# A decoder block on one core: the arithmetic of the early and attention parts moved from GpSimd to VectorE and ScalarE

## The chip, the core and the metric

The kernel runs on one core of a Trainium2 chip. The core has four engines that compute, each with its own instruction queue that it works through in order: TensorE (PE in the profile; its weight loads are a row of their own, PEld), VectorE (DVE), ScalarE (ACT) and GpSimd (POOL). SyncE (SP) issues most transfers. The metric is the device time of one execution in microseconds (us), the median of several runs. One more execution was taken by the profiler; all rows below are of that one.

## The reference, cut to what matters

One decoder block on 256 tokens of width 2048, in float32. Only the first half of it, the token mixer, is touched by the change:

```python
h = rms_norm(x, g_pre_mix) * (1.0 + sc1) + sh1        # sc1, sh1, ... = silu(c) @ w_ada + b_ada
z = h @ w_in                                          # cq, ckv, kr, qs, ks, vs and two gates
o_a = mla_branch(cq, ckv, kr, g_q_lat, w_uq, g_kv_lat, w_ukv)   # 16 heads, rotary part, causal
o_b = swa_branch(qs, ks_, vs, rel_bias, sinks)                  # 32 heads of 64, window 128, sinks
mix = (g_a * o_a + g_b * o_b) @ w_o
x = x + gt1 * rms_norm(mix, g_post_mix)
# then: u = causal_dwconv((rms_norm(x) * (1 + sc2) + sh2) @ w_up); y = (silu(u1) * u2) @ w_down
# apply_rope(x) = x * cos + rotate_half(x) * sin; softmax with a sink adds exp(sink - m) to the sum
```

## The kernel before

Every float32 matrix product is made of three products of rounded halves. A weight tile `raw` of 128 x 1024 arrives by transfer; ACT rounds it to `whi` (L116), DVE subtracts to get the rest `wlo` (L117), and PE multiplies hi by hi, hi by lo and lo by hi (`mm3`, L129 to L131, and variants to L146). Five buffers each of `raw`, `whi` and `wlo` stand between the transfers and PE. The other operand is split in the same way.

The program has these stages. **Early columns** (`early_z`): z for the latents, the keys, the values and the first heads is made in six groups of the 2048 input channels (`KGS` = 2, 2, 2, 2, 4, 4 chunks of 128); the sums over the groups stay in SBUF as twenty tiles `pair` of 128 x 512. For the first group ACT copies a finished PSUM bank (`bk_mm`, three of them) to the pair. For the later ones every third pair (index mod 3 = 1, `PADD`) is copied out by ACT (L373) and added by POOL (L374); the others are added by DVE straight from PSUM (L376). Beside it, modulation columns are made in a background stream: w_ada tiles are multiplied by silu(c) on PE or summed up on DVE (`acc`, L240 and L242). **Hooks in the last group**: `lat` normalises the two latents (sums of squares, L406 on POOL; split, L421 on POOL), `keys` rotates the shared key and splits the keys (L448 to L456 on POOL), `toeplitz` prepares the bias. **Attention**, for eight pairs of heads: `pair_proj` projects queries, keys and values from the latents, and `rope` rotates the queries of two pairs at a time: four products with the sine on 32 partitions each (L434, POOL), one with the cosine (L435, DVE), one sum (L436, POOL). `step` runs one head of MLA and two of the window branch. `stack` puts hi of a 64-row operand on one half of the partitions (L464, ACT) and lo on the other (L465, POOL). Scores go to two PSUM banks (`bk_sc`, L545 to L550); DVE adds mask or bias, takes the maximum and writes to `sm` (L555, two per bank); ACT takes the exponential with its sum (L561); DVE inverts the sum (L563) and multiplies (L566, six per head); PE transposes (L150), ACT copies out (L574), PE multiplies by the values (L578, L583); DVE gates (L586), POOL adds the two branches (L589). `late_z` makes the remaining columns in between. Then come w_o, the second norm, the ConvFFN and the end, which the change doesn't touch.

The order on each engine is fixed before the run: the source calls `tile.TileContext(nc, schedule_with_timeline_sim=True)`, and a scheduler places the instructions of all engines by its own account of them. So a change of engine also moves other instructions in the queues.

Of the kernel before, what the change touches and what calls it, by code (L numbers as in the profile page):

```python
# [10 lines left out]
F32 = mybir.dt.float32  # L11
F32R = mybir.dt.float32r
AF = mybir.ActivationFunctionType
ALU = mybir.AluOpType

P = 128
# [9 lines left out]
NEARLY = 8  # L26
LATS = (3, 4, 5, 6, 7, 8, 9)
HOOKS = (3, 9, 15)
PADD = 3
PUMP = 1.3  # L30
RATES = (0.5, 0.8, 0.3, 0.5)
SPREAD = 7.0
# [11 lines left out]
def block_kernel(ctx: ExitStack, tc: tile.TileContext, a, out: bass.AP):  # L44
# [295 lines left out]
    def early_z(kg, hooks):  # L340
        s, k0 = KGS[kg], k0s[kg]
        nblk = 2048 // (s * P)
        order = []
        for i in range(NPAIR):
            order += [("kr", 6)] if i == 6 else [("vs", 7), ("vs2", 7)] if i == 7 else [(0, i), (1, i)]
        src = a["w_in1"][kg]
        b = None
        for off in range(0, len(order), nblk):
            n = min(nblk, len(order) - off)
            w = n * P * s  # L350
            wt = Weights(src[:, off * P * s:off * P * s + w], w, WT if n == nblk else n * P * (s // 2))
            for u in range(n):
                what, i = order[off + u]
                if what in (0, "kr", "vs"):
                    b = bank("mm")
                if what == "vs":
                    for half in range(2):
                        for kk in range(s):
                            mm3t(b[:, half * T:half * T + T], wt.cut(kk * n * P + u * P, 2 * P), hs[k0 + kk], half,
                                 kk == 0, kk == s - 1)  # L360
                elif what != "vs2":
                    c0 = T if what == 1 else 0
                    for kk in range(s):
                        mm3(b[:, c0:c0 + T], wt.cut(kk * n * P + u * P), hs[k0 + kk], kk == 0, kk == s - 1)
                if what in (1, "kr", "vs2"):
                    wd = T if i == 6 else 2 * T
                    if kg == 0:
                        pairs[i] = blkp.tile([P, 512], F32, tag="blk", name="pair")
                        act.copy(pairs[i][:, :wd], b[:, :wd])
                    elif i % PADD == 1:  # L370
                        pl = xp if kg < len(KGS) - 1 else at
                        part = pl.tile([P, 512], F32, tag="sq" if pl is xp else "tmp", bufs=2, name="part")
                        act.copy(part[:, :wd], b[:, :wd])  # L373
                        pool.tensor_tensor(pairs[i][:, :wd], pairs[i][:, :wd], part[:, :wd], op=ALU.add)  # L374
                    else:
                        dve.tensor_tensor(pairs[i][:, :wd], pairs[i][:, :wd], b[:, :wd], op=ALU.add)  # L376
                    if i in hooks:
                        hooks[i]()
# [19 lines left out]
    def lat(first, npair, width, gofs, res):  # L398
# [4 lines left out]
        for i in range(1, npair):  # L403
            sq = at.tile([P, 512], F32, tag="tmp", name="sq2")
            act.activation(sq, pairs[first + i], AF.Square)
            pool.tensor_tensor(tot, tot, sq, op=ALU.add)  # L406
        for j in range(2):
            pe.matmul(ps[:, :T], ones, tot[:, j * T:j * T + T], start=j == 0, stop=j == 1)
        r = at.tile([P, 512], F32, tag="ropet", bufs=1, name="rl")[:, :T]
# [2 lines left out]
        for i in range(npair):  # L412
# [5 lines left out]
            hi = blkp.tile([P, 512], F32R, tag="blk", name="blk_hi")  # L418
            lo = blkp.tile([P, 512], F32R, tag="blk", name="blk_lo")
            act.copy(hi, pr)  # L420
            pool.tensor_tensor(lo, pr, hi.bitcast(F32), op=ALU.subtract)  # L421
            res += [(hi[:, j * T:j * T + T], lo[:, j * T:j * T + T], None) for j in range(2)]

    def rope(x, n):
# [6 lines left out]

        for q in range(4):
            here, there = slice(32 * q, 32 * q + 32), slice(32 * (q ^ 1), 32 * (q ^ 1) + 32)
            pool.tensor_tensor(t[here], x[there], table(sinT, there), op=ALU.mult)  # L434
        dve.tensor_tensor(x, x, table(cosT, slice(0, P)), op=ALU.mult)  # L435
        pool.tensor_tensor(x, x, t, op=ALU.add)  # L436

    cqn, ckn = [], []

# [3 lines left out]
    def keys():  # L443
# [1 line left out]
        krr = pairs[6][:, :T]  # L445
        rope(krr, 1)
        act.copy(krs[:, 0, :], krr)
        pool.tensor_tensor(krs[:, 1, :], krr, krs[:, 0, :].bitcast(F32), op=ALU.subtract)  # L448
        ksf = at.tile([P, 3, 388], F32, tag="sm", bufs=2, name="ksf").rearrange("p a b -> p (a b)")[:, :4 * T]
        for kv in range(4):  # L450
            src = pairs[5][(kv % 2) * 64:(kv % 2) * 64 + 64, (kv // 2) * T:(kv // 2) * T + T]
            for i in range(2):
                pool.tensor_scalar(down_order(ksf[64 * i:64 * i + 64, kv * T:kv * T + T]), src, -0.125, None, op0=ALU.mult)
        hi = kss[:, 0].rearrange("p k t -> p (k t)")
        act.copy(hi, ksf)
        pool.tensor_tensor(kss[:, 1].rearrange("p k t -> p (k t)"), ksf, hi.bitcast(F32), op=ALU.subtract)  # L456

    def stack(src, tag, w):

# [2 lines left out]
        for e in range(2):  # L462
            me, other = slice(64 * e, 64 * e + 64), slice(64 - 64 * e, 128 - 64 * e)
            act.copy(res[e][me], src[me])  # L464
            pool.tensor_tensor(res[e][other], src[me], res[e][me].bitcast(F32), op=ALU.subtract)  # L465
        return res


# [52 lines left out]
    def step(h):  # L521
# [36 lines left out]
        for i in range(3):  # L558
# [4 lines left out]
            dve.reciprocal(den[:, 2 * i:2 * i + 2], den[:, 2 * i:2 * i + 2])  # L563
            for j, (c0, c1) in enumerate(SEG):
                o, r = sm[:, i, c0:c1], den[:, 2 * i + j:2 * i + j + 1]
                dve.tensor_scalar(o, o, r, None, op0=ALU.mult)  # L566
        ob = bank("o")
        pts = []
        for i in range(3):
# [16 lines left out]
        dve.scalar_tensor_tensor(tm, tg, 1.0, ob, op0=ALU.add, op1=ALU.mult)  # L586
        if e == 0:
            mixs[h // 2] = blkp.tile([P, 512], F32, tag="blk", name="mix")
        pool.tensor_tensor(mixs[h // 2][:, e * T:e * T + T], tm[:, 0:T], tm[:, T:512], op=ALU.add)  # L589

    warm = const.tile([P, 1], F32, name="warm")

# [324 lines left out]
```

## Time and profile before

| | before |
|---|---|
| median of 3 runs | 1502.75 us (1501.55 to 1503.86) |
| profiled execution | 1505.71 us, of which the span 1503.8 us |
| PE busy | 1452.7 us, 97% of the span |
| PEld busy | 1278.0 us, 85% |
| DVE busy | 1083.8 us, 72% |
| ACT busy | 775.6 us, 52% |
| POOL busy | 260.9 us, 17% |
| mean granted clock of PE | 0.988 |

The span is the stretch from the first to the last instruction. The shares are means over stages of different kinds: the early columns last to about 250 us, the last group with its hooks and the attention to about 650 us, and w_o, the norm and the ConvFFN take the rest. A busy PE is modelled from its pipelined matmuls, so 100% is no proof of its peak. The granted clock is the share of TensorE's full speed that the chip allowed.

### The profile page before, as it was taken

What the parts mean: (1) busy time and instruction counts of PE and PEld (TensorE: products, weight loads), DVE (VectorE), ACT (ScalarE), POOL (GpSimd) and SP (SyncE); (2) the same over time, 40 slices, a digit from 0 to 9 for tenths busy, and PEclk for the clock granted to TensorE, in tenths of its full rate; (3) what the DMA queues carried; (4) which work ended last, traced back from release to release, by engine and by line L of the source; (5) the groups of instructions that cost most, each with busy time, mean ns of one, the idle gap of its engine ahead of it and who ended that gap; (6) DMA issues with size and microseconds to landing.
All of it is one profiled execution on the core that took longest, in us unless ns stands there. A gap on an engine that the chain in (4) does not pass through costs nothing.

```text
span 1503.8 us, 24728 instructions
## 1 busy us (share of the span) xinstructions
PE 1452.7 (97%) x9506; PEld 1278.0 (85%) x9506; DVE 1083.8 (72%) x1488; ACT 775.6 (52%) x1223; POOL 260.9 (17%) x191
## 2 busy tenths in 40 slices
PE   7999999889999999999899989999999999999997
PEld 6988899789899998978788878888888888888886
DVE  3579868978887969767788777877767776444443
ACT  4534435545554655755655445655555555434442
POOL 0034315922413425300000000100000000000000
PEclk9999999999999999999899999999999999999999
DMA  9888868588687867659477777765555557555552
GB/s 373 312 313 323 311 233 266 180 272 271 201 298 235 301 228 259 202 201 388 178 243 251 239 253 266 251 209 190 187 190 189 189 190 242 193 195 190 191 193 99
DMA packets 101525, 356.96 MB, mean 237 GB/s; under 512 B 11760, under 2 KB 12208, under 8 KB 100896
## 3 DMA queue, kind: packets, MB, share of 16 engines
q1 hardware_dynamic: 99936, 350.82, 68.4%
q0 software_dynamic: 1472, 4.58, 1.2%
q8 instruction: 74, 1.21, 0.3%
q14 instruction: 43, 0.35, 0.1%
HBM read 351.11 MB, written 4.24 MB: 236 GB/s over the span
## 4 chain that ended last, share of the span: by engine, by line
PE 38%; DMA 10%; DVE 5%; ACT 1%; issue 1%; SPq 0%; DVEq 0%; ACTq 0%
PE bk_mm L136 8%; PE bk_sc L136 6%; DMA raw<-in_w_ada_dram 6%; PE bk_mm L138 4%; PE bk_sc L138 3%; PE bk_mm L144 3%; PE bk_sc L144 3%; PE bk_sc L146 3%; PE bk_mm L146 3%; PE bk_mm L145 3%; PE bk_sc L145 3%; DMA raw<-in_w_up_dram 2%; DVE acc L242 2%; DMA raw<-in_w_o_dram 2%; DVE wlo L117 2%
## 5 line engine op out<-in xcount | busy, mean ns | idle before, releaser
L117 DVE TENSOR_TENSOR wlo<-raw,whi 128x1024 fp32r<-128x1024 f32 (+3 forms) x472 | 594.3, 1266 | 282.8 <-ACT whi L116 280.7
L116 ACT CAST whi<-raw 128x1024 fp32r<-128x1024 f32 (+3 forms) x472 | 478.3, 1021 | 504.8 <-PE bk_mm L130 91.2
L129 PE MATMUL bk_mm<-h,whi 128*128 128x256 f32 x976 | 284.3, 292 | 0.5 <-DVE pair L376 0.5
L131 PE MATMUL bk_mm<-h,wlo 128*128 128x256 f32 x976 | 279.3, 287 | 0.0
L130 PE MATMUL bk_mm<-h,whi 128*128 128x256 f32 x976 | 279.1, 286 | 0.0
L136 PE MATMUL bk_mm<-h,whi 128*128 128x512 f32 x848 | 266.6, 396 | 1.2 <-ACT whi L116 1.2
L242 DVE SCALAR_TENSOR_TENSOR acc<-raw,csil,acc 128x1024 f32<-128x1024 f32 (+1 forms) x141 | 192.1, 1362 | 57.9 <-DMA raw<-in_w_ada_dram 57.3
L129 PEld LDWEIGHTS bk_mm<-h,whi 128*128 128x128 f32 x976 | 187.9, 193 | 16.0 <-issue 11.6
L138 PEld LDWEIGHTS bk_mm<-h,wlo 128*128 128x128 f32 x848 | 158.7, 188 | 44.8 <-DVE wlo L117 7.8
L130 PEld LDWEIGHTS bk_mm<-h,whi 128*128 128x128 f32 x976 | 188.3, 193 | 1.7 <-issue 1.7
L131 PEld LDWEIGHTS bk_mm<-h,wlo 128*128 128x128 f32 x976 | 187.8, 193 | 1.4 <-issue 1.3
L136 PE MATMUL bk_sc<-h,whi 128*128 128x512 f32 x560 | 177.1, 398 | 0.0
L138 PE MATMUL bk_mm<-h,wlo 128*128 128x256 f32 x848 | 167.4, 279 | 4.8 <-DVE wlo L117 4.8
L136 PEld LDWEIGHTS bk_mm<-h,whi 128*128 128x128 f32 x848 | 129.2, 189 | 1.9 <-ACT whi L116 1.4
L138 PEld LDWEIGHTS bk_sc<-h,wlo 128*128 128x128 f32 x560 | 105.4, 189 | 27.3 <-DVE wlo L117 2.6
L761 POOL TENSOR_TENSOR sa<-sa,u 128x512 f32<-128x512 f32 x22 | 33.4, 1520 | 472.8 <-DVE u L755 436.6
L138 PE MATMUL bk_sc<-h,wlo 128*128 128x256 f32 x560 | 110.6, 279 | 1.6 <-DVE wlo L117 1.6
L374 POOL TENSOR_TENSOR pair<-pair,part 128x512 f32<-128x512 f32 x35 | 64.5, 1843 | 190.2 <-ACT part L373 190.1
L136 PEld LDWEIGHTS bk_sc<-h,whi 128*128 128x128 f32 x560 | 85.7, 190 | 0.4 <-issue 0.4
L144 PE MATMUL bk_sc<-whi,g 128*128 128x512 f32 x176 | 68.6, 390 | 0.0
L144 PE MATMUL bk_mm<-whi,g 128*128 128x512 f32 x176 | 68.6, 390 | 0.0
L145 PE MATMUL bk_mm<-wlo,g 128*128 128x512 f32 x176 | 68.5, 389 | 0.0
(197 smaller groups left out, 2261.1 us busy)
## 6 DMA issues: line engine op xcount, KB each, us to landing
raw<-in_w_ada_dram SPq DMA_DIRECT2D x192, 512.0 KB, 5.1
raw<-in_w_up_dram SPq DMA_DIRECT2D x176, 512.0 KB, 4.6
raw<-in_w_in_dram SPq DMA_DIRECT2D x116, 512.0 KB, 5.2
raw<-in_w_down_dram SPq DMA_DIRECT2D x88, 512.0 KB, 4.5
raw<-in_w_o_dram SPq DMA_DIRECT2D x32, 512.0 KB, 5.7
raw<-in_w_uqn_dram SPq DMA_DIRECT2D x16, 384.0 KB, 4.0
bias<-trow POOLq DMA_DIRECT2D x16, 256.0 KB, 4.9
raw<-in_w_ukv_dram SPq DMA_DIRECT2D x16, 256.0 KB, 3.6
```

The costliest lines, as they stand in the source:

```text
L116: act.copy(hi[:, :n], raw[:, :n])
L117: dve.tensor_tensor(lo[:, :n], raw[:, :n], hi[:, :n].bitcast(F32), op=ALU.subtract)
L129: pe.matmul(o, wh, xh, start=start, stop=False)
L130: pe.matmul(o, wh, xl, start=False, stop=False)
L131: pe.matmul(o, wl, xh, start=False, stop=stop)
L136: pe.matmul(o, w[0], x[2], start=start and i == 0, stop=False)
L138: pe.matmul(o[:, :T], w[1], x[0], start=False, stop=stop and i == 1)
L144: pe.matmul(o, ch, wh, start=start, stop=False)
L145: pe.matmul(o, ch, wl, start=False, stop=False)
L146: pe.matmul(o, cl, wh, start=False, stop=stop)
L242: dve.scalar_tensor_tensor(acc[:, :w], r, csil[:, j:j + 1], acc[:, :w], op0=ALU.mult, op1=ALU.add)
L374: pool.tensor_tensor(pairs[i][:, :wd], pairs[i][:, :wd], part[:, :wd], op=ALU.add)
```

## The change

All arithmetic that POOL did up to the end of the attention goes to other engines. The third of the partial sums that took ACT and POOL is now made like the others, by one DVE instruction out of PSUM (so the copies of L373 are gone). The sums of squares, the lo halves of latents and keys, the sine products and sums of the rotation, the stacks' lo halves and the sums of the two branches are now DVE instructions of the same shape. The eight scaled copies in `keys` and the last three of each head's six normalising products go to ACT. POOL keeps the copies of the sinks, its transfers and the product in the ConvFFN (L761).

```diff
-PADD = 3
@@ early_z
-                    elif i % PADD == 1:
-                        pl = xp if kg < len(KGS) - 1 else at
-                        part = pl.tile([P, 512], F32, tag="sq" if pl is xp else "tmp", bufs=2, name="part")
-                        act.copy(part[:, :wd], b[:, :wd])
-                        pool.tensor_tensor(pairs[i][:, :wd], pairs[i][:, :wd], part[:, :wd], op=ALU.add)
                     else:
                         dve.tensor_tensor(pairs[i][:, :wd], pairs[i][:, :wd], b[:, :wd], op=ALU.add)
@@ lat
-            pool.tensor_tensor(tot, tot, sq, op=ALU.add)
+            dve.tensor_tensor(tot, tot, sq, op=ALU.add)
-            pool.tensor_tensor(lo, pr, hi.bitcast(F32), op=ALU.subtract)
+            dve.tensor_tensor(lo, pr, hi.bitcast(F32), op=ALU.subtract)
@@ rope
-            pool.tensor_tensor(t[here], x[there], table(sinT, there), op=ALU.mult)
+            dve.tensor_tensor(t[here], x[there], table(sinT, there), op=ALU.mult)
         dve.tensor_tensor(x, x, table(cosT, slice(0, P)), op=ALU.mult)
-        pool.tensor_tensor(x, x, t, op=ALU.add)
+        dve.tensor_tensor(x, x, t, op=ALU.add)
@@ keys
-        pool.tensor_tensor(krs[:, 1, :], krr, krs[:, 0, :].bitcast(F32), op=ALU.subtract)
+        dve.tensor_tensor(krs[:, 1, :], krr, krs[:, 0, :].bitcast(F32), op=ALU.subtract)
-                pool.tensor_scalar(down_order(ksf[...]), src, -0.125, None, op0=ALU.mult)
+                act.mul(down_order(ksf[...]), src, -0.125)
-        pool.tensor_tensor(kss[:, 1].rearrange("p k t -> p (k t)"), ksf, hi.bitcast(F32), op=ALU.subtract)
+        dve.tensor_tensor(kss[:, 1].rearrange("p k t -> p (k t)"), ksf, hi.bitcast(F32), op=ALU.subtract)
@@ stack
-            pool.tensor_tensor(res[e][other], src[me], res[e][me].bitcast(F32), op=ALU.subtract)
+            dve.tensor_tensor(res[e][other], src[me], res[e][me].bitcast(F32), op=ALU.subtract)
@@ step
-                dve.tensor_scalar(o, o, r, None, op0=ALU.mult)
+                if 2 * i + j < 3:
+                    dve.tensor_scalar(o, o, r, None, op0=ALU.mult)
+                else:
+                    act.mul(o, o, r)
-        pool.tensor_tensor(mixs[h // 2][:, e * T:e * T + T], tm[:, 0:T], tm[:, T:512], op=ALU.add)
+        dve.tensor_tensor(mixs[h // 2][:, e * T:e * T + T], tm[:, 0:T], tm[:, T:512], op=ALU.add)
```

The changed file is shorter, so its line numbers are lower by one (`wlo` is L116 there, `acc` L241) and from `early_z` on by six (L376 becomes L370, L465 becomes L459, L555 becomes L549); the products of L566 are L561 on DVE and L563 on ACT.

How the queues changed is shown at two places. The first is DVE's queue in the last group of early columns, where the latents are normalised (`rl` is the inverse norm, L417 the product with it). Before:

```order
L117 TENSOR_TENSOR wlo<-raw,whi 128x1024
L242 SCALAR_TENSOR_TENSOR acc<-raw,csil,acc 128x1024
L117 TENSOR_TENSOR wlo<-raw,whi 128x768
L411 RECIPROCAL rl<-rl 128x256
L376 TENSOR_TENSOR pair<-pair,bk_mm 128x512
L417 SCALAR_TENSOR_TENSOR pair<-pair,c_gcol,rl 128x256 x4
L117 TENSOR_TENSOR wlo<-raw,whi 128x768
L242 SCALAR_TENSOR_TENSOR acc<-raw,csil,acc 128x1024
```

Now, between the same two pieces of work:

```order
L116 TENSOR_TENSOR wlo<-raw,whi 128x1024 x2
L370 TENSOR_TENSOR pair<-pair,bk_mm 128x512
L405 RECIPROCAL rl<-rl 128x256
L459 TENSOR_TENSOR qs<-pair,qs 64x512
L241 SCALAR_TENSOR_TENSOR acc<-raw,csil,acc 128x1024
L459 TENSOR_TENSOR qs<-pair,qs 64x512
L415 TENSOR_TENSOR blk_lo<-pair,blk_hi 128x512
L370 TENSOR_TENSOR pair<-pair,bk_mm 128x512
L116 TENSOR_TENSOR wlo<-raw,whi 128x1024
L116 TENSOR_TENSOR wlo<-raw,whi 128x768
L370 TENSOR_TENSOR pair<-pair,bk_mm 128x512
L411 SCALAR_TENSOR_TENSOR pair<-pair,c_gcol,rl 128x256 x4
```

The first stacks, a lo half and more of the partial sums, which stood in POOL's queue, are now between the inverse norm and the product with it. The second place is DVE's queue at the second rotation, with the reductions of the next scores (`c_cmask` those of MLA, `bias` those of the window branch; each is two instructions, of which the second reads out the maximum). Before:

```order
L117 TENSOR_TENSOR wlo<-raw,whi 128x1024 x3
L242 SCALAR_TENSOR_TENSOR acc<-raw,csil,acc 128x1024
L555 ISA sm,mx<-bk_sc,c_cmask,c_sink_97 128x128
L555 ISA mx 128x1
L555 ISA sm,mx<-bk_sc,c_cmask,c_sink_97 128x256
L555 ISA mx 128x1
L435 TENSOR_TENSOR ropeq<-ropeq,c_cosT 128x512
L555 ISA sm,mx<-bk_sc,bias,c_sink_97 128x128
```

Now:

```order
L241 SCALAR_TENSOR_TENSOR acc<-raw,csil,acc 128x1024
L428 TENSOR_TENSOR ropet<-ropeq,c_sinT 32x512 x4
L116 TENSOR_TENSOR wlo<-raw,whi 128x1024
L241 SCALAR_TENSOR_TENSOR acc<-raw,csil,acc 128x1024
L429 TENSOR_TENSOR ropeq<-ropeq,c_cosT 128x512
L116 TENSOR_TENSOR wlo<-raw,whi 128x1024
L549 ISA sm,mx<-bk_sc,bias,c_sink_97 128x128
L549 ISA mx 128x1
L549 ISA sm,mx<-bk_sc,bias,c_sink_97 128x256
L549 ISA mx 128x1
L241 SCALAR_TENSOR_TENSOR acc<-raw,csil,acc 128x1024
L430 TENSOR_TENSOR ropeq<-ropeq,ropet 128x512
```

The four sine products stand ahead of the reductions, and the closing sum behind the first two of them.

## Rows read from the trace of the kernel before

**Rows 1.** The chain of work that ended last, in order of time, its earliest piece: start and length in us, what.

```profile
677.38 11.84 DMA raw<-in_w_o_dram
```

**Rows 2.** Busy time of each engine in stretches of the span: stretch, its length, then for each engine busy us and number of instructions, the granted clock of PE, the share of the transfer engines and GB/s.

```profile
50.00:250.00 200.00, 200.00 (x1771) 182.11 (x1772) 155.88 (x193) 87.90 (x116) 60.02 (x33) 1.00 0.83 290
100.00:150.00 50.00, 50.00 (x430) 44.33 (x429) 45.84 (x54) 21.08 (x28) 21.32 (x11) 1.00 0.91 340
250.00:300.00 50.00, 43.26 (x337) 41.96 (x335) 46.65 (x41) 28.85 (x41) 46.84 (x33) 0.97 0.64 197
300.00:350.00 50.00, 43.87 (x340) 42.64 (x341) 41.64 (x60) 27.58 (x55) 16.22 (x12) 0.93 0.81 276
350.00:400.00 50.00, 46.35 (x354) 43.43 (x353) 42.22 (x77) 25.52 (x54) 18.24 (x16) 0.97 0.75 245
400.00:650.00 250.00, 244.85 (x1910) 227.80 (x1910) 207.48 (x387) 141.18 (x310) 81.03 (x66) 0.99 0.75 247
```

The engines stand in the order PE, PEld, DVE, ACT, POOL.

**Rows 3.** What PE waited for from 250 to 650 us: us in total, times, the longest.

```profile
PE bk_sc L550 <- DVE mx L555: 10.5, 5, 4.0
PE bk_mm L129 <- DVE pair L376: 5.2, 4, 2.6
PE bk_mm L145 <- DVE wlo L117: 2.2, 1, 2.2
PE bk_mm L131 <- DVE wlo L117: 1.4, 2, 1.0
PE bk_tp L150 <- DVE sm L566: 1.3, 3, 0.6
```

**Rows 4.** Groups of POOL's instructions over the whole span, shapes apart: line, operation, out<-in, count, then busy us, mean ns of one, and the idle time before them with what ended it.

```profile
L374 POOL TENSOR_TENSOR pair<-pair,part 128x512 f32<-128x512 f32 x35 | 64.5, 1843 | 190.2 <-ACT part L373 190.1
...
L434 POOL TENSOR_TENSOR ropet<-ropeq,c_sinT 32x512 f32<-32x512 f32 x16 | 32.3, 2017 | 34.2 <-ACT ropeq L502 33.5
L465 POOL TENSOR_TENSOR qs<-pair,qs 64x512 fp32r<-64x512 f32 x16 | 27.7, 1734 | 32.1 <-ACT qs L464 31.7
L589 POOL TENSOR_TENSOR mix<-tm 128x256 f32<-128x256 f32 x16 | 21.8, 1365 | 81.1 <-DVE tm L586 81.1
L465 POOL TENSOR_TENSOR qr<-ropeq,qr 64x256 fp32r<-64x256 f32 x16 | 16.5, 1032 | 62.0 <-ACT qr L464 61.5
...
L456 POOL TENSOR_TENSOR kss<-ksf,kss 128x1024 fp32r<-128x1024 f32 x1 | 3.3, 3265 | 0.1
```

**Rows 5.** The same view of DVE from 0 to 250 us.

```profile
L117 DVE TENSOR_TENSOR wlo<-raw,whi 128x1024 fp32r<-128x1024 f32 x59 | 76.4, 1315 | 26.6 <-ACT whi L116 25.8 <-DMA raw<-in_w_in_dram 0.6
L376 DVE TENSOR_TENSOR pair<-pair,bk_mm 128x512 f32<-128x512 f32 x51 | 34.4, 681 | 15.6 <-PE bk_mm L131 15.3
L242 DVE SCALAR_TENSOR_TENSOR acc<-raw,csil,acc 128x1024 f32<-128x1024 f32 x18 | 24.0, 1332 | 4.2 <-DMA raw<-in_w_ada_dram 4.2
...
L376 DVE TENSOR_TENSOR pair<-pair,bk_mm 128x256 f32<-128x256 f32 x4 | 1.7, 413 | 0.0
```

**Rows 6.** The same view of DVE from 640 to 700 us, at the end of the attention and the begin of w_o.

```profile
L117 DVE TENSOR_TENSOR wlo<-raw,whi 128x1024 fp32r<-128x1024 f32 x19 | 22.7, 1221 | 8.0 <-ACT whi L116 7.7
L242 DVE SCALAR_TENSOR_TENSOR acc<-raw,csil,acc 128x1024 f32<-128x1024 f32 x7 | 9.0, 1279 | 8.3 <-DMA raw<-in_w_ada_dram 8.3
L566 DVE TENSOR_SCALAR sm<-sm,den 128x256 f32<-128x256 f32 x6 | 2.1, 350 | 0.0
...
L566 DVE TENSOR_SCALAR sm<-sm,den 128x128 f32<-128x128 f32 x6 | 1.7, 284 | 0.1
L159 DVE TENSOR_TENSOR h<-mix,h 128x512 fp32r<-128x512 f32 x2 | 1.4, 690 | 1.3 <-ACT h L158 1.3
```

**Rows 7.** The same view of DVE from 250 to 650 us.

```profile
L242 DVE SCALAR_TENSOR_TENSOR acc<-raw,csil,acc 128x1024 f32<-128x1024 f32 x75 | 109.3, 1458 | 23.7 <-DMA raw<-in_w_ada_dram 23.2
L117 DVE TENSOR_TENSOR wlo<-raw,whi 128x1024 fp32r<-128x1024 f32 x70 | 98.0, 1407 | 20.4 <-ACT whi L116 20.1
L117 DVE TENSOR_TENSOR wlo<-raw,whi 128x768 fp32r<-128x768 f32 x26 | 29.5, 1139 | 6.0 <-ACT whi L116 6.0
L566 DVE TENSOR_SCALAR sm<-sm,den 128x128 f32<-128x128 f32 x45 | 18.4, 410 | 0.3
L566 DVE TENSOR_SCALAR sm<-sm,den 128x256 f32<-128x256 f32 x44 | 18.2, 414 | 0.0
```

**Rows 8.** Instructions in order of time, DVE's and then POOL's, at the second rotation: start and length in us, then what; the length is that of the whole group where it counts more than one.

```profile
379.46 6.80 DVE L117 TENSOR_TENSOR wlo<-raw,whi 128x1024 fp32r<-128x1024 f32 x3
386.18 2.28 DVE L242 SCALAR_TENSOR_TENSOR acc<-raw,csil,acc 128x1024 f32<-128x1024 f32 x1
...
378.65 8.73 POOL L434 TENSOR_TENSOR ropet<-ropeq,c_sinT 32x512 f32<-32x512 f32 x4 [9.69 <-ACT ropeq L502]
```

**Rows 9.** Groups of ACT's instructions over the whole span, columns as in rows 4.

```profile
L373 ACT COPY part<-bk_mm 128x512 f32<-128x512 f32 x35 | 20.5, 584 | 40.9 <-PE bk_mm L131 21.1 <-PE bk_mm L146 17.2 <-POOL pair L374 1.7
L561 ACT ACTIVATE sm<-sm,mx 128x129 f32<-128x129 f32 x48 | 19.3, 403 | 24.4 <-DVE mx L555 24.3
...
L699 ACT ACTIVATE yg<-x,r 128x512 f32<-128x512 f32 x4 | 2.7, 714 | 0.5 <-DVE r L671 0.5
```

**Rows 10.** Busy time in two microseconds after PE's wait of 2.6 us that ended at 280.7 us, columns as in rows 2.

```profile
281.00:283.00 2.00, 2.00 (x11) 2.00 (x11) 2.00 (x4) 1.33 (x3) 1.99 (x3) 0.50 0.00 0
```

**Rows 11.** POOL's instruction at 335 us, with its idle time before in brackets.

```profile
335.26 0.91 POOL L465 TENSOR_TENSOR qr<-ropeq,qr 64x256 fp32r<-64x256 f32 x1 [11.72 <-ACT qr L464]
```

More of the change, by code (lines that the diff above doesn't have):

```diff
@@ L452, in keys @@
             for i in range(2):
-                pool.tensor_scalar(down_order(ksf[64 * i:64 * i + 64, kv * T:kv * T + T]), src, -0.125, None, op0=ALU.mult)
+                act.mul(down_order(ksf[64 * i:64 * i + 64, kv * T:kv * T + T]), src, -0.125)
         hi = kss[:, 0].rearrange("p k t -> p (k t)")
         act.copy(hi, ksf)
-        pool.tensor_tensor(kss[:, 1].rearrange("p k t -> p (k t)"), ksf, hi.bitcast(F32), op=ALU.subtract)
+        dve.tensor_tensor(kss[:, 1].rearrange("p k t -> p (k t)"), ksf, hi.bitcast(F32), op=ALU.subtract)
     def stack(src, tag, w):
```

## The prediction

> **What bounds the kernel now.** I read the chain of work first. It can be followed back from the end only to 677.38 us [rows 1], and everything the diff touches stands before that, so the chain says nothing on the change and the stretch before it has to be read from windows. The windows [rows 2] give the busy time of each engine. From 50 to 250 us TensorE (PE) is busy 200.00 of 200 us: it bounds that stretch, with VectorE (DVE) at 155.88. From 250 to 650 us PE is idle 6.74 + 6.13 + 3.65 + 5.15 = 21.7 us, and its granted clock falls to 0.97, 0.93 and 0.97 in the three windows up to 400 us. That is where something can be won. Meanwhile DVE is busy 46.65 + 41.64 + 42.22 + 207.48 = 338.0 of 400 us and GpSimd (POOL) 162.3; from 250 to 300 us both are busy for over 46 of 50 us. Who ends PE's idle time is in the waits [rows 3]: DVE in every row shown, 10.5 us at the score matmuls (L550) for a score bank that the reductions of L555 must empty, 5.2 at L129 for the sums of L376, 3.6 for wlo, 1.3 for the normalising products. So the attention part runs on PE, and PE is held up by an in-order DVE queue that is 85% full.
>
> **What the change adds to DVE.** 118 instructions leave POOL for DVE. The large groups are in [rows 4]; the small ones follow from the code (5 subtractions and 3 sums of squares in lat(), 4 closing sums of the rotation, and of 256 columns 4 products, 1 sum and 1 split in keys()). By width: 35 + 16 + 16 + 5 + 4 + 3 = 79 of 512 columns, 16 + 16 + 6 = 38 of 256, one of 1024. DVE needs 681 ns for a sum of 512 columns out of PSUM and 413 for 256 [rows 5], 690 for a 512-column subtraction with both inputs in SBUF and 1221 for one of 1024 [rows 6]. I take 0.68, 0.42 and 1.22: 53.7 + 16.0 + 1.2 = **70.9 us**. The sin products work on 32 partitions and the stacks on 64; what so few partitions, or an output on other partitions than the inputs, cost on DVE is in no row. On POOL the products took 2017 ns and the stacks 1734, a full tile 1843 [rows 4], so I price by columns, with 6% less and 9% more as the bounds: of 30 us for 52 such instructions, 28 to 33.
>
> **What it takes off DVE.** First, products 4 to 6 of the six of each head go to ScalarE (ACT): 32 of 256 and 16 of 128 columns at 350 and 284 ns [rows 6], 15.7 us. Second, and larger, DVE's own work gets shorter. The same instruction has two prices: wlo of 1024 columns takes 1221 ns on average where POOL is nearly idle [rows 6] and 1407 from 250 to 650 us [rows 7]; one stretch shows why [rows 8]: four sin products on POOL take 8.73 us, and the three wlo beside them 6.80, 2.27 each, the acc behind them 2.28 instead of 1.28. [...] Sums out of PSUM are not slowed: 681 ns in the early stretch with POOL at 60 of 200 us. From 250 to 650 us the excess is 70 x 0.186 (wlo of 1024) + 26 x 0.184 (wlo of 768, at 0.955 between the 512 and 1024 prices) + 75 x 0.179 (acc) + 45 x 0.126 + 44 x 0.064 (products) = 13.0 + 4.8 + 13.4 + 5.7 + 2.8 = 39.7 us. Before 250 us it is 59 x 0.094 + 18 x 0.053 = 6.5 us [rows 5]. With no arithmetic on POOL I let all of it go, **46.2 us**; the other bound is that none goes because something else (the transfers) causes it, against which stand rows 8, where the slow ones begin and end with the POOL group.
>
> [...]
>
> Net on DVE: 70.9 - 15.7 - 46.2 = **+9 us**, but unevenly. Before 250 us: 30 partial sums and 2 sums of squares, 21.8 - 6.5 = +15.3, to 171 of 200 us. From 250 to 650 us: 49.1 - 14.6 (89 of the 96 products stand there) - 39.7 = -5.2, to 333 of 400; the rest of the products lies behind. So DVE is relieved a little where PE waits, and loaded where PE does not wait.
>
> **ACT** loses 35 copies of 584 ns (20.5 us) [rows 9] and gains 48 products and 8 scaled copies in keys(). A product by a column on ACT is shown for 512 columns only, 714 ns [rows 9]; between that and the 403 of the exponential of 129 columns I take 0.48 and 0.38 for 256 and 128, 21 us, and 0.4 for the eight, 3 us. Net +4 us on an engine that is busy 223 of 400 us: hidden by its idle time, and worth nothing by itself. POOL keeps the sink copies and the bias transfers, which no longer queue behind sums.
>
> **What PE gets back**, by the waits. (a) L129 and wlo, 5.2 + 2.2 + 1.4 = 8.8 us. The windows show POOL and DVE full there. The order shows that the subtractions and sin products now stand in the same DVE queue, so of the relief only half is left: 4.4. (b) The score banks, 10.5. At 385 us [rows 8] DVE reaches the reduction after 9.1 us of three wlo and an acc; at the undisturbed prices 4.9, and now four sin products of 0.68 stand before it, so it comes 1.4 us sooner. The longest, 4.0 [rows 3], ends at 336 us, where POOL had been idle for 11.72 us [rows 11], and stays; of the other 6.5 half: 3.2. (c) The products, 1.3: half, 0.7. Sum 8.3. [...]
>
> **What it costs PE.** Before 250 us PE has no wait to speak of, and the partial sums now sit between PE and its three banks. ACT copied a bank out on its own; now DVE must, behind whatever it has. From 100 to 150 us DVE is busy 45.84 and gets 11 x 0.68 - 2.3 (its share of the 6.5) = 5.2 more: 51.0 of 50, 1 us too much. The five wlo buffers run ahead of PE and hide the rest (without that cover the whole 15.3 would show). I charge 1.0 and as much again for banks that come free late: 2.0.
>
> Sum: -8.3 - 2.5 + 2.0 = **-8.8 us** on the profiled execution's 1505.71 us (span 1503.8 and 1.9 around it), 1496.9. That execution is 3.0 us above the median of the runs, so 1502.75 - 8.8 = **1494.0 us**.
>
> **Rivals.** R1, more than that: DVE's order is planned ahead and POOL's slowing of DVE is what puts it behind that plan; with it gone nearly all waits go, 21.7 + 6.5 - 2 = -26, 1476.5. For it: at 385 us POOL alone had put DVE 4.1 us behind. Against: the wait that ends at 336 us, and DVE still at 83%. R2, no change that counts: PE's waits move to other places of a DVE queue that is as full as before, 1500 to 1505. For it: the net of +9 us. R3, slower: the score reductions wait behind the moved work, in one queue. Place: the four rotations that feed a stack (2.7 us of sin products and 0.7 of sum each) and the eight stacks (2.2 us each), 31 us put ahead of reductions or wlo on which PE waits. With half of it uncovered, +15.6 - 8.8 = +7, 1509.6; it decides from the point where more than 28% (8.8 of 31) is uncovered. For it: DVE ends every wait of rows 3. Against: on POOL the same work already held up DVE for 39.7 us. [...]
> R4 is a part of R3 in mechanism but on ACT: products there wait for reciprocals from DVE and casts wait behind them. ACT already waits 24.3 us for reductions in 48 cases [rows 9], 0.5 each; 32 more such waits are 16 us against 177 us of idle time, so alone it costs at most a few us.
>
> **Chances.** Forecast (3 to 17 us faster) 0.44; R1 0.15; R2 0.18; R3 with R4 0.23. A difference under 0.2%, 3 us, can't be told from none: faster 0.59, same 0.18, slower 0.23. Leaving out the outer part of R1 and R3, one in ten each, the range is 1480 to 1510; the forecast alone has 1486 to 1500.
>
> **What would show it.** Right: wlo and acc from 250 to 650 us at 1.22 and 1.28 us; moved sums at 0.68; PE's waits for DVE there at some 13 us instead of 21, and a granted clock nearer 1.00 up to 400 us; before 250 us PE still busy throughout. Wrong: wlo still at 1.4 (the excess was not POOL's); PE idle before 250 us (banks); waits of L550 over 10 us, ended by reductions behind sin products or stacks (R3); casts late behind products on ACT (R4).

## The result, and the profile after

The changed kernel takes **1478.93 us** (median of 4 runs, 1475.61 to 1481.65), the kernel before 1503.3 beside it: a ratio of 0.9838, 95% interval 0.9818 to 0.9858, 24.4 us faster. The forecast was 8.8 us faster, 1494.0 with a range from 1480 to 1510, so the time lies below the range, and close to the number of rival R1 (1476.5). The profiled execution took 1481.65 us, its span 1479.9.

The windows first, columns as in [rows 2].

```profile
50.00:250.00 200.00, 198.50 (x1787) 181.79 (x1786) 164.70 (x226) 71.97 (x86) 0.52 (x1) 1.00 0.83 288
...
250.00:300.00 50.00, 44.10 (x341) 42.68 (x340) 44.63 (x61) 27.84 (x44) 2.03 (x4) 0.97 0.61 197
300.00:350.00 50.00, 48.46 (x395) 45.80 (x393) 47.91 (x95) 34.58 (x78) 3.60 (x4) 1.00 0.85 283
350.00:400.00 50.00, 50.00 (x408) 48.49 (x406) 41.07 (x64) 29.51 (x56) 2.29 (x4) 1.00 0.81 282
400.00:650.00 250.00, 248.15 (x1896) 227.91 (x1896) 209.68 (x409) 159.77 (x352) 11.40 (x20) 1.00 0.78 257
```

TensorE's idle time from 250 to 650 us went from 21.7 to 9.3 us, and its granted clock from 0.93 and 0.97 to 1.00 between 300 and 400 us. GpSimd does almost nothing. VectorE is as busy as before, 343 of 400 us for 338, and it does more in them.

What TensorE waited for from 250 to 650 us, columns as in [rows 3]:

```profile
PE bk_mm L130 <- DVE wlo L116: 4.5, 2, 4.0
PE bk_o L575 <- ACT pT L571: 1.7, 2, 0.9
PE bk_mm L128 <- DVE pair L370: 1.2, 2, 1.0
PE bk_mm L143 <- ACT whi L115: 0.9, 1, 0.9
PE bk_mm L128 <- ACT whi L115: 0.6, 1, 0.6
```

The largest row of before, 10.5 us for score banks, is gone altogether, and so are the normalising products. VectorE's groups in the same stretch, columns as in [rows 7]: the first three are the ones slowed before, then moved work at its new price.

```profile
L241 DVE SCALAR_TENSOR_TENSOR acc<-raw,csil,acc 128x1024 f32<-128x1024 f32 x76 | 97.3, 1281 | 7.0 <-DMA raw<-in_w_ada_dram 6.4
L116 DVE TENSOR_TENSOR wlo<-raw,whi 128x1024 fp32r<-128x1024 f32 x77 | 93.7, 1223 | 23.5 <-ACT whi L115 23.3
L116 DVE TENSOR_TENSOR wlo<-raw,whi 128x768 fp32r<-128x768 f32 x26 | 24.8, 957 | 8.9 <-ACT whi L115 8.9
...
L459 DVE TENSOR_TENSOR qs<-pair,qs 64x512 fp32r<-64x512 f32 x16 | 11.0, 689 | 0.5
L428 DVE TENSOR_TENSOR ropet<-ropeq,c_sinT 32x512 f32<-32x512 f32 x16 | 10.9, 683 | 0.6 <-ACT ropeq L496 0.3
```

The low part of 1024 columns went from 1407 to 1223 ns, acc from 1458 to 1281 [rows 7]: these are the undisturbed prices. One place shows what that does. Before, the four sin products of the second rotation took 8.73 us on GpSimd, with three low parts of 2.27 us each beside them [rows 8]. Now, in order of time on VectorE:

```profile
369.35 2.77 DVE L428 TENSOR_TENSOR ropet<-ropeq,c_sinT 32x512 f32<-32x512 f32 x4 [0.30 <-ACT ropeq L496]
372.15 1.23 DVE L116 TENSOR_TENSOR wlo<-raw,whi 128x1024 fp32r<-128x1024 f32 x1
```

The same products take a third of the time on VectorE, and what follows is not slowed. The other half of the normalising products, on ScalarE from 250 to 650 us, columns as in [rows 9]:

```profile
L563 ACT ACTIVATE sm<-sm,den 128x256 f32<-128x256 f32 x32 | 16.1, 505 | 0.2 <-DVE den L557 0.2
...
L563 ACT ACTIVATE sm<-sm,den 128x128 f32<-128x128 f32 x16 | 6.4, 399 | 0.1
```

They hardly wait.

**A measure used below.** For every VectorE instruction I take its time less the median time of the same shape in the trace after, where that is positive, and add these up from 250 to 700 us; I call the sum the *slowing*. It is 43.8 us before and 1.1 after. Losses in us are differences of two ratios to the kernel before, times 1503; each ratio is uncertain by 0.001 to 0.003, so such a difference by some 4 us. *First scores* are the first score matmuls of the window branch (`bk_sc<-kss,qs`). Start and length in us, before and then after:

```profile
327.02 0.63 PE L550 MATMUL bk_sc<-kss,qs 128*128 128x128 f32 x4
```

```profile
302.99 0.70 PE L544 MATMUL bk_sc<-kss,qs 128*128 128x128 f32 x4
```

### The profile page after: what moved, and what is told of

The parts are those of the page before. It is cut to its first block, busy times and chain, and to the rows that moved or that the text cites. A ratio compares the mean times of both kernels' runs of the same rounds, so it can differ in the third digit from the quotient of the medians.

```text
span 1479.9 us, 24583 instructions
## 1 busy us (share of the span) xinstructions
PE 1442.6 (97%) x9506; PEld 1271.2 (86%) x9506; DVE 1082.0 (73%) x1558; ACT 777.6 (53%) x1242; POOL 56.9 (4%) x65
## 4 chain that ended last, share of the span: by engine, by line
PE 79%; DMA 10%; DVE 7%; issue 2%; ACT 2%; DVEq 0%; SPq 0%; ACTq 0%
PE bk_mm L135 11%; PE bk_sc L135 8%; PE bk_mm L128 7%; PE bk_mm L130 7%; PE bk_mm L129 7%; DMA raw<-in_w_ada_dram 6%; PE bk_mm L137 6%; PE bk_mm L143 4%; PE bk_mm L144 4%; PE bk_mm L145 4%; PE bk_sc L137 4%; PE bk_sc L143 3%; PE bk_sc L145 3%; PE bk_sc L144 3%; DVE acc L241 2%
## 5 line engine op out<-in xcount | busy, mean ns | idle before, releaser
L116 DVE TENSOR_TENSOR wlo<-raw,whi 128x1024 fp32r<-128x1024 f32 (+3 forms) x472 | 567.7, 1209 | 275.2 <-ACT whi L115 272.5
L241 DVE SCALAR_TENSOR_TENSOR acc<-raw,csil,acc 128x1024 f32<-128x1024 f32 (+1 forms) x141 | 177.4, 1258 | 36.4 <-DMA raw<-in_w_ada_dram 35.7
L370 DVE TENSOR_TENSOR pair<-pair,bk_mm 128x512 f32<-128x512 f32 (+1 forms) x100 | 65.6, 673 | 19.0 <-PE bk_mm L130 15.0
L143 PE MATMUL bk_mm<-whi,g 128*128 128x512 f32 x176 | 68.6, 390 | 0.0
L145 PE MATMUL bk_mm<-whi,g 128*128 128x512 f32 x176 | 68.5, 389 | 0.0
```

The source lines that it names most:

```text
L116: dve.tensor_tensor(lo[:, :n], raw[:, :n], hi[:, :n].bitcast(F32), op=ALU.subtract)
L143: pe.matmul(o, ch, wh, start=start, stop=False)
L145: pe.matmul(o, cl, wh, start=False, stop=stop)
L241: dve.scalar_tensor_tensor(acc[:, :w], r, csil[:, j:j + 1], acc[:, :w], op0=ALU.mult, op1=ALU.add)
```

## The experiments

The theory to test (T): VectorE was slowed by GpSimd's reading and therefore came late to what TensorE waited for. Its rivals: GpSimd's results were themselves late (L); the new order of the instructions is the gain (O); the products on ScalarE are the gain (P).

### GpSimd reads beside the changed kernel, with nobody waiting for it

The room for a scratch tile comes from one of the 24 blocks of 512 columns; a_nblk has just that change.

```
-NBLK = 24
+NBLK = 23
 # a_read, after the copy of the sinks in step(h):
+        with tc.issue_after(cp.ins):
+            for n, w in ((64, 512), (64, 256), (128, 256), (32, 512)) + (((128, 512),) if h % 4 == 0 else ()):
+                j = jo[:n, :w].rearrange("p (o t) -> p o t", t=T)
+                pool.tensor_tensor(j, of(cosT, n, w), of(sinT, n, w), op=ALU.add)
 # a_write, instead:
+                for _ in range(3):
+                    pool.memset(j, 1.0)
```

> The changed kernel with one buffer less in the pool of 512-column blocks (23 for 24), which makes room for the scratch tile of the next two runs; on every engine but GpSimd its order of instructions is the same as theirs, so it is what they are compared with. Every theory: 1477 to 1484 us, the blocks being no limit of the changed kernel (1478.9).

> The same, and GpSimd does per attention step four additions (64x512, 64x256, 128x256, 32x512, and 128x512 in every fourth step) on two constant tables into a scratch tile that nobody reads: the shapes of the arithmetic that the change took off GpSimd in the attention, with no result for anyone to wait for. Theory T (the 24 us came from VectorE no longer being slowed, so that it keeps to its order in time): about 70 to 100 us of GpSimd reading beside VectorE, which by the kernel before (162 us of GpSimd slowed VectorE by 39.7) costs VectorE 17 to 25 us, and most of the attention's gain of 20 us goes: 10 to 20 us above the run without the additions, with the wait for score banks back. Rival L (the gain is the end of GpSimd's own late results) and rival O (the gain is the new order of instructions): within 2 us of the run without.

> The same scratch tile, but GpSimd writes it with memsets (three for each addition, about as long in all) and reads nothing. [...] If any GpSimd work at all slows VectorE, or if the later bias transfers behind the additions are what costs: as slow as the run with additions.

Measured: a_nblk 1488.25 us (ratio 0.9894, interval 0.9868 to 0.9921), a_read 1512.67 (1.0054, 1.0036 to 1.0073), a_write 1487.99 (0.9886, 0.9867 to 0.9905). On VectorE and ScalarE the three have the same instructions in the same order, all 1558 and 1242 of them. GpSimd's additions in a_read (first two groups), and its memsets in a_write (third row), from 250 to 650 us; columns as in [rows 4]:

```profile
L541 POOL TENSOR_TENSOR jo<-c_cosT,c_sinT 32x512 f32<-32x512 f32 x15 | 27.2, 1813 | 1.2
L541 POOL TENSOR_TENSOR jo<-c_cosT,c_sinT 64x512 f32<-64x512 f32 x15 | 23.5, 1568 | 0.1
```

```profile
L542 POOL MEMSET jo<- 64x512 f32 x48 | 25.6, 533 | 1.8
```

VectorE in a_read, then in a_nblk, then in a_write (one row), same stretch:

```profile
L116 DVE TENSOR_TENSOR wlo<-raw,whi 128x768 fp32r<-128x768 f32 x26 | 30.8, 1189 | 2.4 <-ACT whi L115 2.4
L460 DVE TENSOR_TENSOR qs<-pair,qs 64x512 fp32r<-64x512 f32 x16 | 15.4, 963 | 0.5
L569 DVE TENSOR_SCALAR sm<-sm,den 128x128 f32<-128x128 f32 x28 | 14.4, 513 | 0.3
```

```profile
L116 DVE TENSOR_TENSOR wlo<-raw,whi 128x768 fp32r<-128x768 f32 x26 | 24.7, 953 | 5.6 <-ACT whi L115 5.6
L459 DVE TENSOR_TENSOR qs<-pair,qs 64x512 fp32r<-64x512 f32 x16 | 11.0, 686 | 0.5
L561 DVE TENSOR_SCALAR sm<-sm,den 128x128 f32<-128x128 f32 x32 | 8.9, 280 | 0.3
```

```profile
L116 DVE TENSOR_TENSOR wlo<-raw,whi 128x768 fp32r<-128x768 f32 x26 | 24.6, 950 | 5.6 <-ACT whi L115 5.5
```

And TensorE's waits in a_read from 250 to 650 us, then the one for score banks in a_nblk:

```profile
PE bk_mm L130 <- DVE wlo L116: 9.7, 3, 6.8
PE bk_sc L552 <- DVE mx L557: 7.1, 6, 2.7
PE bk_o L583 <- ACT pT L579: 4.7, 3, 2.0
PE bk_tp L149 <- DVE sm L569: 2.3, 4, 0.8
```

```profile
PE bk_sc L544 <- DVE mx L549: 2.9, 1, 2.9
```

Reading that nobody waits for costs 24 us, more than the 10 to 20 expected, and brings back waits for score banks (7.1 us for 2.9) and for products; writing for as long (102.5 us of GpSimd busy from 250 to 650 us, for 107.7) costs nothing that can be measured, 1487.99 us for 1488.25, as T has it, which names reading alone. The slowing is 42.9 us in a_read, as in the kernel before, 2.9 in a_write and 0.4 in a_nblk. That is theory T by itself: L and O can't make the difference between these three. The low parts of 768 columns, which have two inputs in SBUF, took 1189 ns in a_read, 950 in a_write and 953 in a_nblk. The block less was not free as I had expected: 8.4 us by the ratios (9.3 by the medians), with the first scores at 329.7 us for 303.0. Its windows, columns as in [rows 2]:

```profile
250.00:300.00 50.00, 45.37 (x328) 43.88 (x326) 45.70 (x62) 28.28 (x44) 2.03 (x4) 0.90 0.65 208
300.00:350.00 50.00, 45.03 (x338) 43.74 (x338) 40.02 (x65) 23.84 (x46) 0.72 (x1) 0.90 0.78 252
```

From 250 to 650 us TensorE is idle 9.6 us, nearly as in the changed kernel (9.3). The loss is in the granted clock: 0.90 in both windows for 0.97 and 1.00, (0.07 + 0.10) x 50 = 8.5 us.

### GpSimd keeps its place in the kernel before, but hardly reads

```
+    def gp(o, x, y, op):       # in place of pool.tensor_tensor
+        pool.tensor_tensor(c(o), c(x), c(y), op=op)   # c: 16 columns of each row
+        o = o.bitcast(F32) if o.dtype == F32R else o
+        for _ in range(3):
+            pool.memset(o, 0.5)
```

> The kernel before, where each of GpSimd's tensor-tensor operations of the early and attention parts (not the eight scaled copies of the keys) reads 16 columns of its operands only and then writes its output three times over with memsets: GpSimd stands in every chain as before and is occupied nearly as long (about 1.8 us for 2.0 at 512 columns), but hardly reads; VectorE has the same instructions as before, in nearly the same order. The outputs are left out by this (they hold constants). Theory T (VectorE slowed by GpSimd's reading): most of the gain appears without any work moved, 18 to 30 us faster than before, 1474 to 1486; the low part of 1024 columns falls from 1407 to about 1222 ns between 250 and 650 us. Rival L (it was GpSimd's late results, in the chain from the rotated queries to the scores): 1500 to 1505, no change. Rival O (the new order): 1498 to 1505.

Measured: 1484.99 us (ratio 0.9878, 0.9848 to 0.9908): 18 us faster than before, with no work moved to VectorE. (GpSimd's results are constants here, so only the times count.) GpSimd's whole busy time from 250 to 650 us was 182.5 us, more than the 162.3 of before, and at the second rotation it is 12.2 us from the first sine product to the end of the sum, for 12.5. VectorE, then TensorE's waits, then the busy times as in [rows 2], in that stretch:

```profile
L251 DVE SCALAR_TENSOR_TENSOR acc<-raw,csil,acc 128x1024 f32<-128x1024 f32 x76 | 97.2, 1279 | 24.7 <-DMA raw<-in_w_ada_dram 24.1
L117 DVE TENSOR_TENSOR wlo<-raw,whi 128x1024 fp32r<-128x1024 f32 x76 | 93.0, 1226 | 29.2 <-ACT whi L116 26.0 <-PE bk_sc L559 1.6 <-PE bk_tp L150 1.0
```

```profile
PE bk_mm L131 <- DVE wlo L117: 3.6, 1, 3.6
PE bk_o L592 <- ACT pT L583: 1.6, 1, 1.6
PE bk_sc L559 <- DVE mx L564: 1.2, 1, 1.2
```

```profile
250.00:650.00 400.00, 391.61 (x3033) 365.48 (x3032) 312.61 (x588) 235.84 (x478) 182.54 (x382) 1.00 0.77 255
```

Rival L falls as the main cause: GpSimd is as late as before, and three quarters of the gain (18.3 of 24.4) are there. So does O: 1411 of VectorE's 1488 instructions stand in the order of before, and the first scores come at 321.6 us. The other 6.0 us, between this kernel and the changed one, may be GpSimd's longer chain, the 6.2 us of slowing that are left, or the order; the runs don't part these. The trace can't show them: the profiled execution was the fastest of its four (1479.56 of up to 1489.08 us), and TensorE is idle 8.4 us in it, less than the 9.3 of the changed kernel.

### Parts of the change, alone and undone

```
 # b_prod: before, with          # a_prod: after, all six on VectorE
+if 2 * i + j < 3: dve.tensor_scalar(...)   else: act.mul(o, o, r)
 # b_rs: before, rope() and stack() on dve      # a_rot: after, rope() on pool
 # a_mix: after, mixer sums on pool             # a_psum: after, partial sums on pool
 # a_ffn: after, with
-            pool.tensor_tensor(sa, sa, us[1], op=ALU.mult)
+            dve.tensor_tensor(sa, sa, us[1], op=ALU.mult)
```

> The kernel before with one part of the change alone: three of the six normalising products of each step on ScalarE. It takes 15 to 20 us off VectorE (these products are among the operations that GpSimd slows) and adds as many to ScalarE. Theory T with VectorE behind its order by some 40 us: a part of the gain, 4 to 10 us faster (1494 to 1500). Rival P (the products on ScalarE are the gain): 15 us or more faster. The forecast's own account, which gives a freed us of VectorE half a us: 8 us faster.

> The changed kernel with all six normalising products on VectorE: VectorE, now not slowed, gets 48 products of 0.28 and 0.37 to 0.40 us back, 15.7 us. Theory T: VectorE then has about as much work as it has time between 250 and 650 us (333 + 16 of 400), so a little: 1 to 6 us slower than the changed kernel (1480 to 1485). Rival P: 15 us slower, near 1495.

> The kernel before with the rotation and the stacks on VectorE, 53 instructions; partial sums, latents, keys and mixer sums stay on GpSimd. These are the operations that stand between a projection and the scores, and about 90 of the 162 us that GpSimd is busy between 250 and 650 us. Rival L: nearly all of the gain, 1478 to 1484. Theory T by share of GpSimd's busy time: 90/162 of 20 us, 1490 to 1494.

> The changed kernel with the rotation's products and sum back on GpSimd (25 instructions, about 45 us of GpSimd at the durations of before). Theory T by share: 45/162 of 20 us, 4 to 7 us slower than the changed kernel. Rival L: the rotation is 9.5 us of GpSimd in a row for every two pairs, ahead of the scores of both: the first scores come 10 us or more later (313 for 303 us), and 8 us or more are lost in all.

> The changed kernel with the mixer sums back on GpSimd (16 instructions, about 20 us of GpSimd beside VectorE, whose results TensorE needs only much later). Theory T by share: 20/162 of 20 us, 2 to 3 us slower than the changed kernel (1481 to 1482). Rival L: no loss, 1477 to 1480.

> The changed kernel with the partial sums of the first products back on GpSimd (35 of the 118 moved instructions, 30 of them before 250 us). Theory T: the gain arose after 350 us, so 1477 to 1482 us. Rival E (VectorE's new early load costs what the first projection started late, 285.5 for 280.7 us): 3 to 5 us faster, 1474 to 1476. The forecast's early loss of 2.0 us: 1477. If the early part gave its share of the 24 us: 1485 or more.

> The changed kernel with the last arithmetic of GpSimd, the 22 products of the feed-forward part, on VectorE too: no arithmetic on GpSimd at all. Theory T: the low part of 1024 columns goes from 1253 to 1222 ns between 760 and 960 us, VectorE gets 22 products of 0.69 us more, TensorE's waits for low parts there are 3 us; between 1 us slower and 3 us faster, 1475 to 1480.

| kernel | median us | ratio to before, interval | slowing, us | loss against the changed kernel, us |
|---|---|---|---|---|
| a_psum | 1478.38 | 0.9820, 0.9800 to 0.9839 | 3.1 | -2.7 |
| a_prod | 1477.49 | 0.9830, 0.9806 to 0.9853 | 0.5 | -1.2 |
| a_ffn | 1479.40 | 0.9829, 0.9809 to 0.9849 | 0.5 | -1.4 |
| a_mix | 1478.96 | 0.9839, 0.9821 to 0.9858 | 4.0 | 0.2 |
| b_rs | 1484.04 | 0.9875, 0.9854 to 0.9896 | 14.7 | 5.6 |
| a_rot | 1490.62 | 0.9923, 0.9900 to 0.9947 | 17.8 | 12.8 |
| b_prod | 1503.31 | 1.0001, 0.9988 to 1.0014 | 43.0 | 24.5 |

The products on ScalarE are worth nothing that can be told from noise, in either kernel: P falls. So does my own account in b_prod: it took 15 us of work off VectorE (323 us busy from 250 to 650 us for 338), and the waits for score banks stayed as they were, because the slowing did. TensorE's first wait in b_prod, VectorE's price of a low part there, and the busy times from 250 to 650 us in b_prod and then in a_prod:

```profile
PE bk_sc L550 <- DVE mx L555: 11.4, 6, 3.4
```

```profile
L117 DVE TENSOR_TENSOR wlo<-raw,whi 128x1024 fp32r<-128x1024 f32 x70 | 97.7, 1404 | 24.6 <-ACT whi L116 24.6
```

```profile
250.00:650.00 400.00, 380.11 (x2932) 357.50 (x2931) 323.15 (x517) 238.80 (x500) 157.08 (x124) 0.97 0.74 241
```

```profile
250.00:650.00 400.00, 392.78 (x3055) 366.97 (x3054) 357.16 (x678) 234.71 (x480) 17.65 (x30) 1.00 0.78 256
```

a_prod is the counterpart: 48 products more on VectorE (357 us busy for 343), no loss. Some 15 us more or less of VectorE's work was not what TensorE waited for. The partial sums, which bring most of the new early work, and the mixer sums make no difference that can be told, on either engine. With the partial sums back on GpSimd (a_psum), VectorE is slowed by 9.4 us before 250 us, for 0.8 in the changed kernel, and nothing is lost: TensorE hardly waits there. The rotation and the stacks carry most of the gain: b_rs has 18.8 of the 24.4 us with 57 of the 118 instructions (53, as expected above, is a miscount).

By the share of GpSimd's busy time theory T missed three times, and L's numbers came nearer: in b_rs (1490 to 1494 us expected), a_mix (2 to 3 us lost) and a_rot (4 to 7 us lost). Busy time was the wrong key. By the slowing measured, b_rs (5.6 us lost at 14.7 us) and a_mix (0.2 at 4.0) are in line with a_half below (7 at 16.4). a_rot is not: it lost 12.8 us at 17.8 us of slowing. Its first scores stand at 325.9 us, as in the kernel before (327.0) and not at 303.0; L had foreseen them 10 us late. Here a late result and the slowing seem to come together; no run parts them. Without the feed-forward part's products on GpSimd the low parts there go from 1253 to 1221 ns, as expected, and the time doesn't move: TensorE had 3 us of waits to lose there.

### How much slowing, and where

```
 # a_half: half of a_read's additions
-            for n, w in ((64, 512), (64, 256), (128, 256), (32, 512)) + ...
+            for n, w in ((64, 512), (64, 256)) if h % 2 else ((128, 256), (32, 512)):
 # a_early: a_read's additions behind the bias transfer, not behind the copy of the sinks
 # a_blk25: 24 blocks become 25, the rotation's temporary in tag "tmp"
 # b_again: the kernel before, unchanged
```

> The changed kernel with 23 blocks and half of GpSimd's additions into the scratch tile: in even steps those of 128x256 and 32x512, in odd ones 64x512 and 64x256. All of them slowed VectorE by 42.9 us between 250 and 700 us and made the kernel 24.4 us slower. Theory T: about 21 us of slowing, and 10 to 14 us above the run with 23 blocks and no additions: 1498 to 1502. If there is a point below which slowing is free (the forecast halved the waits, but took VectorE to have 60 of 400 us to spare): under 5 us, below 1493.

> The changed kernel with 23 blocks and all of the additions, put behind each step's bias transfer in GpSimd's queue, which waits for the reductions of two steps before, and not behind the copy of the sinks, which waits for the transposes of two steps before. The same GpSimd work, earlier in the step. Theory T if only the sum of VectorE's slowing counts: about 40 us of slowing, 1508 to 1516, as before. If it counts which VectorE instructions are slowed (the mixer sums on GpSimd cost nothing, the rotation 12 us): another time, 1495 to 1506 or over 1516, at a like sum of slowing.

> The changed kernel with one block more (25), the room for it taken from the rotation's own temporary tile, which goes into the pair of 512-column temporaries. One block less cost 9.3 us, whose order had the first scores at 330 us for 303. If the blocks hold back the order of work: 1472 to 1477; if 24 are enough: 1478 to 1480; if the rotation now waits for a temporary: slower than 1481.

> The kernel before once more, for a second profile of it. Of the 24 us, 19.6 are won by the transposes of the attention's result (739.1 us before, 719.4 after), and another 4.6 between these and the feed-forward part's 100th low part later on (268.5 us before, 264.3 after). If the 4.6 belong to the change (its order of instructions, or GpSimd's products there), this profile shows 268 to 269 us again; if the one execution profiled before was late there by chance, 263 to 265, as in the experiments so far, of which one differs from the kernel before by the three products alone.

Measured: a_half 1492.76 us (ratio 0.9939, 0.9923 to 0.9954) at 16.4 us of slowing; a_early 1519.21 (1.0117, 1.0098 to 1.0136) at 44.8; a_blk25 1481.46 (0.9865, 0.9845 to 0.9885), no better than 24 blocks; b_again 1502.25.

Against a_nblk the loss is 7 us at 16.4 us of slowing, 24 at 42.9, 34 at 44.8. At the rate of a_read 16.4 us would cost 9, which these runs can't tell from 7: neither a price in proportion nor a little free room is excluded. (T had expected 10 to 14 for 21 us of slowing, of which 16.4 came; free room under 5.) The same sum at an earlier place costs 10 us more. In a_early the reading falls on the products between the exponentials and the transposes, and TensorE waits for them, 11.9 us for 2.3 in a_read; VectorE's group and TensorE's first wait there:

```profile
L569 DVE TENSOR_SCALAR sm<-sm,den 128x128 f32<-128x128 f32 x27 | 20.9, 775 | 0.2
```

```profile
PE bk_tp L149 <- DVE sm L569: 11.9, 9, 3.9
```

GpSimd's copies of the sinks come later in a_early too, so a part of its 10 us may be theirs.

b_again gives a second profile of the kernel before. In the first, 19.6 of the 24 us were won by the transposes that follow the attention and w_o (739.1 us before, 719.4 after) and 4.4 behind them. In the second these transposes begin at 742.6 us, 23.1 later than after, and from there to the end of the span it takes 760.9 us, as in the changed kernel (760.4; it was 764.8). So the piece behind was that one execution's; the gain lies ahead of the transposes, in the attention part. TensorE's first wait in the second profile, from 250 to 650 us:

```profile
PE bk_sc L550 <- DVE mx L555: 11.2, 4, 4.9
```

## Why the prediction was wrong

**What held.** The seat of the gain (250 to 650 us), the cause (GpSimd's reading slows VectorE) and its size: 39.7 us of slowing from 250 to 650 us, against 43.8 by the measure above. All but 1.1 of it went, as taken. The prices: moved sums 683 to 691 ns for 512 columns and 420 for 256, on 32 and 64 partitions too; products on ScalarE at 505 and 399 ns for an estimated 480 and 380, with 0.2 us of waits for reciprocals, so R4 did not come. From 50 to 250 us TensorE idles 1.5 us, for which 2.0 was charged, though only 0.6 of it is for a bank, which was the reason given; 0.9 is for rows from ScalarE.

**The step that failed is "What PE gets back".** There I let half of each wait return, "so of the relief only half is left", since the moved work stands in the same queue. Where TensorE waited for score banks all of it came back, and of the clock most. In stalls (from one matmul's start to the next, those over 0.4 us, less 0.24 each, twice the median of 0.12) TensorE lost 24.0 us from 250 to 700 us before, and 9.5 after. In 15 of the 22 stalls before, VectorE's unbroken run of work that ended in the stall held more slowing than the stall was long, and these 15 are 16.1 of the 24.0 us. That count is a bound: stalls close together share a run, and in the second profile (b_again) it is 13 of 21 stalls and 13.6 of 29.7 us. The direct sign is b_noread2: with 6.2 us of slowing left, no work moved and nearly the same order, the stalls are 8.6 us. Term by term: (a) sums and low parts 8.8 us, 4.4 expected back, 3.1 came back (5.7 left, of which 4.0 is one new wait). (b) score banks 10.5, 3.2 expected, all 10.5 came; this is the largest miss. (c) products 1.3, 0.7 expected, 1.3 came. (d) the clock: no run shows the 2.5 us of the forecast's sum; it was an estimate of mine, the 8.3 of 21.7 us of waits taken as a share of what the windows of [rows 2] lost to the granted clock, (0.03 + 0.07 + 0.03) x 50 = 6.5 us, which R1 has whole. After, they lost 0.03 x 50, so 5.0 came back: from 300 to 400 us the granted clock is now 1.00. The stretch from 400 to 650 us, which the forecast left out, went from 0.99 to 1.00, another 2.5 by the rounded rows. Stalls and clock are 14.5 + 5.0 to 7.5 = 19.5 to 22 us, for 19.6 that the first profile shows up to the transposes.

**"The longest, 4.0 ... stays"** was wrong, though its reason was right. VectorE's run before that wait holds 0.00 us of slowing, and the wait is there without any slowing in a_nblk (2.9 us, ending at 338 us). In both, one more low part stands ahead of the reduction on VectorE and waits for ScalarE; before, it is this one:

```profile
334.36 1.23 DVE L117 TENSOR_TENSOR wlo<-raw,whi 128x1024 fp32r<-128x1024 f32 x1 [1.15 <-ACT whi L116]
```

In b_noread2 the reduction stands ahead of that low part and the same stall is 0.2 us; in the changed kernel, with its first scores at 303.0, there is none. So this piece goes by the place in the queue, not by the slowing: 4.0 of the 10.5 us came back for a reason that the forecast didn't have.

**The price of the moved work** was put in the wrong currency. The net of +9 us on VectorE's busy time counted a us of slowing and a us of work alike. b_prod and a_prod show that some 15 us of work more or less make no difference, while a_read shows that 43 us of slowing cost 24. Planned work is laid out by the scheduler in an order that suits it; slowing comes on top in bursts, some 4 us at a time beside the rotation [rows 8], and what stands behind it in VectorE's queue can be late by that much. That the planner's part is the reason is my reading; what is shown is the difference in price.

R1 had this right, "DVE's order is planned ahead and POOL's slowing of DVE is what puts it behind that plan", at a chance of 0.15. That its 26 us came so near to 24.4 is in part luck: it let nearly all of the 21.7 us of idle time go, and 9.3 are left. I held against it the wait at 336 us, which had another cause, and VectorE's 83%, which a_prod shows to be no limit. R3's 31 us of rotations and stacks ahead of reductions cost nothing to be seen: in the changed kernel no wait for score banks is left.

**What stays open:** how the 6.0 us between b_noread2 and the changed kernel divide, why the clock is lower in a_nblk with hardly more idle time, and how much of the 24.4 us is owed to the earlier scores: a_nblk, with late ones and no slowing, is 8.4 us slower than the changed kernel, but a block less is not only an order.

## What to carry to other kernels

Look in the trace for one instruction with two prices, as the low part of 1024 columns here, 1407 and 1223 ns; the surplus over the lower one, added up, is time put in front of what stands behind it in that queue, and here it weighed more than the same time of planned work: 43 us of it cost 24 (a_read), 15 us of planned work nothing that can be told (b_prod, a_prod). Price it by the stalls that end such a burst, and not by the queue's busy share. Work on a helper engine that cost nothing here could stay where it is: the memsets (1487.99 us for 1488.25), the partial sums, which fall where TensorE hardly waits (1478.38 for 1478.93), and the mixer sums, which slow VectorE little (4.0 us; 1478.96).

## What the runs showed of the hardware

GpSimd's memsets left instructions with two SBUF inputs alone: wlo of 1024 columns took 1221 ns in a_write and 1226 in b_noread2, for 1223 in the changed kernel. The normalising products, which have one, took longer beside them: 330 ns at 128 columns in a_write for 280 in a_nblk, 411 at 256 columns in b_noread2 for 352 in a_prod. Beside the reading of a_read it was 513 at 128 columns, and in [rows 7] 410, for 284 in [rows 6]. A VectorE operation on 32 or 64 partitions took as long as on 128: in the changed kernel 683 (L428), 689 (L459) and 691 ns (L430) at 512 columns.
